# One hybrid decoder layer on one core: ScalarE and VectorE in program order through the mixer stage

## The chip, the core and the metric

The kernel runs on one core of a Trainium2 chip. Five engines of the core take part, each with its own row of instructions: TensorE (PE, matmuls; the profile shows its weight loads apart, as PEld), ScalarE (ACT), VectorE (DVE), GpSimd (POOL) and SyncE (SP, which issues nearly all transfers). An engine takes its row in the order in which it was built; an instruction that waits for a semaphore holds what stands behind it in that row. The metric is the time of one execution on the device in microseconds; lower is better. Two runs of the kernel before gave 2639.35 and 2638.07 us, median 2638.71.

## What is computed

One decoder layer (DEPTH is 1) over 2048 tokens of width 1024, all in float32. An input projection feeds two groups of four heads: gated DeltaNet (GDN) and HGRN2. Their outputs go through one output projection, then a squared-ReLU MLP, then a gated per-layer embedding. The gated delta rule solves a triangular system in each chunk of 64 tokens and carries a state of 128x128 from chunk to chunk; HGRN2 carries a state with a decay of its own for every row. The reference, cut to what matters:

```python
hn = rms_norm(h, pre_mix_norm[i])
proj = jnp.einsum('btd,dc->btc', hn, w_in[i]).astype(f32)
...
qkv = jax.nn.silu(causal_depthwise_conv(qkv, gdn_conv[i].astype(f32)))
q_a, k_a, v_a = jnp.split(qkv, 3, axis=-1)
...
o_a = gated_delta_rule_chunked(q_a, k_a, v_a, g_dec, beta)
o_a = gated_head_norm(o_a, gdn_norm[i], z_gdn)
...
log_f = jnp.logaddexp(jax.nn.log_sigmoid(f_pre), jnp.log(lb) + jax.nn.log_sigmoid(-f_pre))
k_b = (1.0 - lb) * jax.nn.sigmoid(-f_pre)
o_b = hgrn2_chunked(jax.nn.silu(q_hg), k_b, i_hg, log_f)
o_b = gated_head_norm(o_b, hgrn_norm[i], g_hg)
...
mix_out = jnp.einsum('btc,cd->btd', mix, w_out[i])
h = h + rms_norm(mix_out, post_mix_norm[i])

u = jnp.einsum('btd,df->btf', rms_norm(h, pre_mlp_norm[i]), w_mlp_up[i])
y = jnp.einsum('btf,fd->btd', jnp.square(jax.nn.relu(u)), w_mlp_down[i])
h = h + rms_norm(y, post_mlp_norm[i])

e = rms_norm(jnp.einsum('bte,ed->btd', p[i], w_ple_proj[i]), ple_norm[i])
gate = jax.nn.sigmoid(jnp.einsum('btd,de->bte', h, w_ple_gate[i]))
h = h + e * gate
```

## The kernel before

Every large float32 product is made of three matmuls on split operands: `split` (L174) writes a rounded copy of an array with ScalarE (L176, a copy) and the remainder with VectorE (L177, a subtraction that needs the copy), and TensorE multiplies high by high, high by low and low by high. `split_in_place` (L227) does the same where the array stands already (L229, L230).

The stages follow each other: a prologue (part of the embedding, the first input operands), the mixers, the output projection, the MLP, the gate. The change concerns the mixers. There the 2048 tokens are taken in four **quarters** of 512 tokens (index q, 0 to 3). In each quarter TensorE works through 33 **works**: a small one for the decay inputs, then for each of four heads h eight projections of 128 columns (`KINDS`: GDN's k, q, z and v, then HGRN2's f, i, q and g). A work is 24 matmuls of 128x512 on the input weights `w` and the input operands `xt` (L1176). In quarter 0 the weights of a work come raw from memory, are split and are kept in memory in split form (`stage_work`, `split_work`, `keep_work`, L1073 to L1086: transfers `raw`, then L176 and L177 on `w`, then `cache_in`); quarters 1 to 3 load the split form back (`reload`).

A clock of **ticks** ties the heads to the works. A work has three ticks of eight matmuls each (`SPT`), with a half-tick between. `tick` (L382) and `half` (L387) advance the generators that stand in `agenda` for that moment. `gdn_mixer` (L635) and `hgrn_mixer` (L857) are such generators: each `yield` ends a step, and the tables `A_STEPS` and `B_STEPS` (L56, L60) say at which tick, counted from the head's first work, a step is stated. So while TensorE projects one head, the scans of the head before are worked off in small pieces. In the GDN mixer the pieces that matter below are a triangular solve (`pr` and `xs`, L746 and L748, a chain of 30 VectorE instructions per head in which each needs the one before) and the recurrence over four chunks (`psa` on TensorE, `r` on VectorE L822, `psb` on TensorE, `w_g` on ScalarE L827, `psc` on TensorE, the new state `S_g` on VectorE L832). In the HGRN2 mixer there are seven levels; at each, VectorE scales the keys (L928), ScalarE copies them for TensorE (`keys`, L931), VectorE scales the queries (L932) and puts TensorE's product `at_all` into `att` (L933). Towards a quarter's end `load_x` (L1087) scales and splits the next quarter's operands `xt` (L1097, L176, L177), and `down_sums` forms sums of MLP weights. After the last quarter `early_outs` (L1047) begins the output projection (`mmo`) with its weights `w_out`.

Who sets the order in which an engine's instructions stand: inside `tc.manual_schedule(engines=...)` the named engines take them in the order in which the program states them; for every other engine the scheduler of the framework orders them by its own estimate of when their inputs are ready. TensorE is in program order in the whole kernel (L324). The prologue has SyncE, ScalarE and VectorE in program order too (L394). The mixer loop (L1156) has SyncE alone beside TensorE.

Of the kernel before, what the change touches and what calls it, by code (L numbers as in the profile page):

```python
# [96 lines left out]
def trunk(ctx, tc, x, xT, pT, vecs, w_in, w_ab, gdn_a_log, gdn_dt_bias, w_out, w_up, w_down,  # L97
# [13 lines left out]
    def bank(name, pool=None):  # L111
        return (pool or pm).tile([P, QT], F32, tag="ps", name=name)
# [269 lines left out]
    def tick():  # L382
        for gen in agenda.pop(clock[0], ()):
            next(gen, None)
        clock[0] += 1

    def half():  # L387

        for gen in agenda.pop(clock[0] - 0.5, ()):
            next(gen, None)  # L390
# [72 lines left out]
    with mixers as mctx:  # L463
# [60 lines left out]
        def decays(ps, q):  # L524

            sp = m2.tile([4, QT], F32, tag="tmp", name=f"sp_{q}")
            se = m2.tile([4, QT], F32, tag="th", name=f"se_{q}")
            S.activation(sp, ps[0:4, :], AF.Identity, bias=dec[:, 1:2])
            S.activation(gb[32:36, :], ps[32:36, :], AF.Tanh, scale=0.5)
            V.tensor_scalar(gb[32:36, :], gb[32:36, :], 0.5, 0.5, ALU.mult, ALU.add)  # L530
            V.scalar_tensor_tensor(se, sp, -1.0, sp, ALU.mult, ALU.max)
            S.activation(se, se, AF.Exp, scale=-1.0)
            S.activation(se, se, AF.Ln, bias=1.0)
            V.scalar_tensor_tensor(sp, sp, 0.0, se, ALU.max, ALU.add)
            V.tensor_scalar(sp, sp, nexpa, None, ALU.mult)
            for c in range(NC):
                V.tensor_tensor_scan(gb[0:4, blk(c)], one[0:4, :], sp[:, blk(c)], 0.0, ALU.mult, ALU.add)
            gd = dr.tile([4, QT], F32, name=f"gd{q}")
            decay[q] = [gd, None]
            yield  # L540
            nc.sync.dma_start(gd, gb[0:4, :])
            yield
            back = mt(f"gbb_{q}", "gbb", 1, (36, QT // 2))
            V.tensor_copy(back.rearrange("p (n b i) -> p n b i", b=NB, i=SB), odd_back(gb))
            yield
            ps = bank(f"ps_gb_{q}", ph)
            for c in range(NC):
                PE.transpose(ps[:, c * 36 : (c + 1) * 36], back[:, blk(c // 2)] if c % 2 else gb[:, blk(c)],
                             ident[:36, :36])
            gcol = sm.tile([P, NC, 36], F32, tag="gcol", name=f"gcol_{q}", bufs=2)  # L550
            V.tensor_copy(gcol.rearrange("p c n -> p (c n)"), ps[:, : NC * 36])
            V.tensor_scalar(gcol[:, :, 4:8], gcol[:, :, 0:4], -1.0, None, ALU.mult)
            decay[q][1] = gcol
# [459 lines left out]
        def at(t, gen, offsets):  # L1013
            for o in offsets:
                agenda.setdefault(t + o, []).append(gen)
# [31 lines left out]
        def early_outs():  # L1047

            for j, (q, d) in enumerate(order):
                for n in range(3, len(tile_of)):  # L1050
                    if ready_at(n) == j:
                        at(clock[0], ready_halves(n), (0, 1))
                for n in range(5, len(tile_of)):
                    if stage_at(n) == j:
                        stage_out(n)
                ps, w = bank(f"mmo_{q}_{d}"), ready[load_of[j]]
                for i in range(3 * KD):
                    k, term = i // 3, i % 3
                    PE.matmul(ps, w[:, term // 2, k, :], xin[q][k][:, term % 2, :], start=i == 0, stop=i == 3 * KD - 1)  # L1059
                    if i % 4 == 3 and i + 1 < 3 * KD:  # L1060
                        yield
                        while i > KD and held_y:
                            nc.sync.dma_start(*held_y.pop())
                y = m2.tile([P, QT], F32, tag="ld", name=f"yo{q}_{d}", bufs=2)
                S.activation(y, ps, AF.Copy)
                square_sums[q] = squares(square_sums[q], ps, d, f"o{q}")
                finished.append(j)
                held_y.append((yod[q][d], y))
                yield
# [3 lines left out]
        def stage_work(j):  # L1073

            if j < len(works) and works[j][3] == 0:
                staged[j] = stage(works[j][0], works[j][2])

        def split_work(j):

            if j < len(works):  # L1080
                split_w[j] = staged.pop(j)() if j in staged else reload(works[j][1], works[j][0])

        def keep_work(j):
            if works[j][3] == 0:
                keep(works[j][1], split_w[j])
# [67 lines left out]
        for q in range(2):  # L1153
            at(0, norm_steps(accs[q], 1.0 / D, EPS, f"e{q}", partial(ple_r.__setitem__, q)),
               [4 * q + i for i in (0, 2, 4, 5, 6)])
        with tc.manual_schedule(engines={mybir.EngineType.SP}):  # L1156
            stage_work(0)
            stage_work(1)
            split_work(0)
            stage_work(2)  # L1160
            split_work(1)
            for j, (name, key, src, q, h, then, g, b) in enumerate(works):
                split_work(j + 2)
                stage_work(j + 3)
                keep_work(j)
                ps = bank(f"mm_{name}")
                w, xt = split_w.pop(j), xts[q]
                terms = []
                for k, xk in enumerate(xt):
                    terms += [(w[:, 0, k, :], xk[:, 0, :]), (w[:, 0, k, :], xk[:, 1, :]), (w[:, 1, k, :], xk[:, 0, :])]  # L1170
                nt = len(terms)
                for s in range(SPT):
                    for i in range(s * nt // SPT, (s + 1) * nt // SPT):
                        if i == (2 * s + 1) * nt // (2 * SPT):
                            half()
                        PE.matmul(ps, *terms[i], start=i == 0, stop=i == nt - 1)  # L1176
                    if s == SPT - 1 and h is None:
                        at(clock[0], decays(ps, q), (0, 2, 3, 5) if q else (0, 2, 4, 7))
                    tick()
                    if s == SPT - 1 and h is not None:  # L1180
                        then(ps, q, h, g, b)

            outs = early_outs()
            while clock[0] <= last or len(finished) * SPT < clock[0] - end:
                next(outs)
                half()
                next(outs)
                tick()
            outs.close()
            nc.sync.dma_start(*held_y.pop())  # L1190
# [798 lines left out]
```

## Time and profile before

| | |
|---|---|
| median of two runs | 2638.71 us |
| span of the profiled execution | 2639.5 us |
| mixer loop, about | 46 us to 1030 us |
| VectorE busy over the span | 74% |
| ScalarE busy over the span | 55% |
| loads of ScalarE's function tables | 68 |

The profiled execution's own time is its span, 2639.5 us; it lies 0.15 us over the slower of the two runs, so nothing of weight lies around it. The page gives the busy time of each engine, the span in 40 slices of 66 us, the chain that ended last, and groups of instructions by line. Views of the trace used below are the busy time by stretch, the waits (which engine waited for what, in total, how often, longest), one line's instructions, and the timeline. In a row such as "128x512 f32 x3072 | 785.5, 401 | 1.6" stand the shape, the count, busy us in all and ns of one, and the engine's idle time before them. Matmuls overlap, so their mean is longer than the distance between them.

### The profile page before, as it was taken

The numbers are of one execution on the slowest core, as the hardware profiler recorded it, in microseconds if no ns is written. First come the engines' busy times: TensorE is split into PE (matmuls) and PEld (weight loads), VectorE is DVE, ScalarE is ACT, GpSimd is POOL, SyncE is SP. The second block draws the span as 40 slices with busy tenths as digits, with TensorE's granted clock in tenths as the row PEclk, the third lists the DMA queues.
The fourth block names the chain that finished last, engine by engine and source line by source line (L and its number), as shares of the span: only waits on it lengthen the run. The fifth ranks groups of instructions, "written<-read, shape, count | busy, mean of one in ns | idle before, by whom it ended". The sixth has DMA issues, their size and how long they took to land.

```text
span 2639.5 us, 43913 instructions
## 1 busy us (share of the span) xinstructions
PE 2602.8 (99%) x15593; PEld 2146.0 (81%) x15593; DVE 1965.0 (74%) x4032; ACT 1463.3 (55%) x2991; POOL 137.0 (5%) x147
## 2 busy tenths in 40 slices
PE   8999999999999999999999999999999999999999
PEld 6778788878878888787888888888888888888887
DVE  7778777776777777579988768767877765477775
ACT  7766655465555555566666465555454465565431
POOL 0000000000000000110000000001000001101000
PEclk9999999999999999999999999999999999999999
DMA  8877777767767675764675576665644375677663
GB/s 277 282 258 265 263 256 245 238 222 251 241 213 240 222 237 162 232 203 141 214 236 182 179 233 223 214 211 186 220 150 168 140 245 187 202 252 251 207 223 126
DMA packets 267788, 573.87 MB, mean 217 GB/s; under 512 B 55578, under 2 KB 60152, under 8 KB 250416
## 3 DMA queue, kind: packets, MB, share of 16 engines
q1 hardware_dynamic: 265264, 566.86, 64.5%
q0 software_dynamic: 2304, 4.20, 0.9%
q8 instruction: 123, 2.02, 0.3%
q14 instruction: 97, 0.79, 0.1%
HBM read 410.57 MB, written 160.37 MB: 216 GB/s over the span
## 4 chain that ended last, share of the span: by engine, by line
PE 61%; DMA 2%; issue 2%; DVE 2%; ACT 0%; POOL 0%; SPq 0%; DVEq 0%; POOLq 0%; ACTq 0%
PE d L1210 23%; PE u L1210 23%; PE mmg L1210 7%; PE mm L1176 4%; PE mmo L1059 1%; PE mme L203 1%; DMA yod<-yo 1%; DMA mixT<-mixd 0%; DMA rsb_g<-rd_g 0%; DMA yo<-in_xT_dram 0%; DVE t L177 0%; DMA rd_g<-m_g 0%; DVE acc_o L246 0%; POOL yo L1296 0%; DMA raw_out<-in_w_out_dram 0%
## 5 line engine op out<-in xcount | busy, mean ns | idle before, releaser
L1176 PE MATMUL mm<-xt,w 128*128 128x512 f32 x3072 | 785.5, 401 | 1.6 <-DVE acc_vg L571 0.7
L1176 PEld LDWEIGHTS mm<-xt,w 128*128 128x128 f32 x3072 | 552.8, 188 | 108.3 <-issue 2.1
L1210 PE MATMUL d<-db,da 128*128 128x512 f32 x2688 | 612.8, 389 | 0.0
L1210 PE MATMUL u<-t,wu 128*128 128x512 f32 x2604 | 591.2, 389 | 0.0
L1210 PEld LDWEIGHTS d<-db,da 128*128 128x128 f32 x2688 | 504.5, 188 | 104.8
L1210 PEld LDWEIGHTS u<-t,wu 128*128 128x128 f32 x2604 | 488.7, 188 | 101.5
L230 DVE TENSOR_TENSOR db<-db 128x512 fp32r<-128x512 f32 x224 | 159.5, 712 | 60.0 <-ACT db L229 59.0
L1612 DVE TENSOR_TENSOR u<-u,u 128x512 f32<-128x512 f32 x224 | 150.2, 681 | 52.0 <-PE u L1210 50.4
L229 ACT ACTIVATE db<-db 128x512 fp32r<-128x512 f32 x224 | 140.9, 629 | 67.4 <-DMA db<-hid 63.6
L1210 PE MATMUL mmg<-h2T,wg 128*128 128x512 f32 (+1 forms) x792 | 174.7, 383 | 0.0
L1210 PEld LDWEIGHTS mmg<-h2T,wg 128*128 128x128 f32 x792 | 145.5, 188 | 29.1
L1655 ACT ACTIVATE u<-u 128x512 f32<-128x512 f32 x128 | 80.7, 631 | 152.8 <-DVE u L1612 152.1
L177 DVE TENSOR_TENSOR da<-da 128x512 fp32r<-128x512 f32 x128 | 95.2, 743 | 91.3 <-ACT da L176 89.5
L176 ACT ACTIVATE da<-da 128x512 fp32r<-128x512 f32 x128 | 80.6, 630 | 127.8 <-DMA da<-sumd 100.9
L1210 PE MATMUL mmo<-mixT,w_out 128*128 128x512 f32 x600 | 140.0, 393 | 3.3 <-ACT w_out L176 2.0
L1210 PEld LDWEIGHTS mmo<-mixT,w_out 128*128 128x128 f32 x600 | 113.4, 190 | 28.8 <-DVE w_out L177 2.6
L176 ACT ACTIVATE wu<-a 128x512 fp32r<-128x512 f32 x124 | 75.0, 623 | 55.8 <-DMA a<-in_w_up_dram 52.9
L177 DVE TENSOR_TENSOR wu<-a,wu 128x512 fp32r<-128x512 f32 x124 | 85.9, 694 | 8.3 <-ACT wu L176 8.2
L177 DVE TENSOR_TENSOR da<-dr,da 128x512 fp32r<-128x512 f32 x96 | 68.2, 711 | 23.7 <-ACT da L176 22.2
L1656 ACT ACTIVATE u<-u 128x512 f32<-128x512 f32 x128 | 80.4, 628 | 3.0
L176 ACT ACTIVATE da<-dr 128x512 fp32r<-128x512 f32 x96 | 60.5, 630 | 31.9 <-DMA dr<-in_w_down_dram 21.7
L246 POOL TENSOR_TENSOR acc_y<-acc_y,sq_y 128x512 f32<-128x512 f32 x28 | 37.8, 1351 | 759.5 <-ACT sq_y L245 759.5
(401 smaller groups left out, 3675.4 us busy)
## 6 DMA issues: line engine op xcount, KB each, us to landing
w<-cache_in SPq DMA_DIRECT2D x96, 1024.0 KB
db<-hid SPq DMA_DIRECT2D x224, 256.0 KB
cache_in<-w SPq DMA_DIRECT2D x32, 1024.0 KB
hid<-u SPq DMA_DIRECT2D x128, 256.0 KB
da<-sumd SPq DMA_DIRECT2D x128, 256.0 KB
a<-in_w_up_dram SPq DMA_DIRECT2D x124, 256.0 KB
hid<-ht SPq DMA_DIRECT2D x96, 256.0 KB
dr<-in_w_down_dram SPq DMA_DIRECT2D x96, 256.0 KB
```

The lines of the kernel that those rows point to most:

```text
L176: S.activation(t[:, 0], raw, AF.Copy)
L177: eng.tensor_tensor(t[:, 1], raw, t[:, 0], ALU.subtract)
L203: PE.matmul(ps, a, b, start=i == 0, stop=i == n - 1)
L229: S.activation(t[:, 0], plain(t), AF.Copy)
L230: V.tensor_tensor(t[:, 1], plain(t), t[:, 0], ALU.subtract)
L246: eng.tensor_tensor(acc, acc, sq, ALU.add)
L1059: PE.matmul(ps, w[:, term // 2, k, :], xin[q][k][:, term % 2, :], start=i == 0, stop=i == 3 * KD - 1)
L1176: PE.matmul(ps, *terms[i], start=i == 0, stop=i == nt - 1)
L1210: PE.matmul(ps, a, b, start=start, stop=stop)
L1612: V.tensor_tensor(c[new], c[old], ps, ALU.add)
L1655: S.activation(c[k], c[k], AF.Relu)
L1656: S.activation(c[k], c[k], AF.Square)
```

## The change

One line: the mixer loop's scope names ScalarE and VectorE beside SyncE. Nothing is computed otherwise; no tile, buffer, transfer or step table is touched.

```diff
-        with tc.manual_schedule(engines={mybir.EngineType.SP}):
+        with tc.manual_schedule(engines={mybir.EngineType.SP, mybir.EngineType.Activation, mybir.EngineType.DVE}):
             stage_work(0)
             stage_work(1)
             split_work(0)
```

TensorE's row is the same instruction for instruction. ScalarE's and VectorE's rows hold the same instructions, among them 68 table loads as before, in another order through the mixer loop. GpSimd's and SyncE's rows change at a handful of places, for in the rest of the kernel the scheduler goes on from another state.

**ScalarE in quarter 0, second head's projections.** `w_16_0_1` is the split weight of the work that projects HGRN2's f for head 1; `keys_h0_0_2` and so on are the key copies of levels 2 and up of head 0. Before:

```order
L580 ACTIVATE y_qg0_1_1322<-acc_qg0_1_1315 128x512
L787 ACTIVATE part5_586<-psp5_g0_0_1395 32x2x32 x4
L931 ACTIVATE keys_h0_0_3_1417<-qk_h0_0_1011 128x2x8x16
L606 ACTIVATE zt_zg0_1_1426<-mm_12_0_1_1330 128x512
L685 ACTIVATE q2_g0_1_1494<-y_qg0_1_1322 128x512
L931 ACTIVATE keys_h0_0_4_1488<-qk_h0_0_1011 128x2x4x32
L176 ACTIVATE w_16_0_1_1323<-raw_16_0_1_1251 128x1024
```

and with the change:

```order
L567 ACTIVATE acc_qg0_1_1315<-mm_0_0_1_1255,cols_96 128x512
L568 ACTIVATE hist_581<-mm_0_0_1_1255 128x3
L176 ACTIVATE w_16_0_1_1323<-raw_16_0_1_1251 128x1024
L931 ACTIVATE keys_h0_0_2_1348<-qk_h0_0_1011 128x2x16x8
L500 ACTIVATE xs1_0_0_1265,ss2_x1_1264<-xs1_0_0_1265 128x512
L669 ACTIVATE jk_g0_1_0_1374,ssk_g0_1_1365<-t_kg0_1_1368 128x128
```

The weight's copy moved ahead, in front of three key copies behind which it stood.

**VectorE at the same place.** `att_h0_0` is the score array of head 0, `u_g0_1` and `qk_g0_1` belong to the GDN solve of head 1. Before:

```order
L932 TENSOR_TENSOR qk_h0_0_1011<-qk_h0_0_1011,gg_h0_0_2_1352 128x2x16x8
L933 COPY_PREDICATED att_h0_0_1207<-cst_93,at_all_81 128x2x16x8
L928 TENSOR_TENSOR qk_h0_0_1011<-qk_h0_0_1011,gg_h0_0_3_1421 128x2x8x16
L928 TENSOR_TENSOR qk_h0_0_1011<-qk_h0_0_1011,gg_h0_0_4_1492 128x2x4x32
L177 TENSOR_TENSOR w_16_0_1_1323<-raw_16_0_1_1251,w_16_0_1_1323 128x1024
L799 COPY xn_g0_0_1233<-psx5_g0_0_1459 32x2x32 x2
L932 TENSOR_TENSOR qk_h0_0_1011<-qk_h0_0_1011,gg_h0_0_3_1421 128x2x8x16
```

and with the change:

```order
L572 TENSOR_TENSOR acc_qg0_1_1315<-acc_qg0_1_1315,bound_582 128x3
L177 TENSOR_TENSOR w_16_0_1_1323<-raw_16_0_1_1251,w_16_0_1_1323 128x1024
L928 TENSOR_TENSOR qk_h0_0_1011<-qk_h0_0_1011,gg_h0_0_1_1302 128x2x32x4
L932 TENSOR_TENSOR qk_h0_0_1011<-qk_h0_0_1011,gg_h0_0_1_1302 128x2x32x4
L933 COPY_PREDICATED att_h0_0_1207<-cst_93,at_all_81 128x2x32x4
L939 TENSOR_TENSOR gg_h0_0_2_1352<-gg_h0_0_1_1302 128x64
L928 TENSOR_TENSOR qk_h0_0_1011<-qk_h0_0_1011,gg_h0_0_2_1352 128x2x16x8
L932 TENSOR_TENSOR qk_h0_0_1011<-qk_h0_0_1011,gg_h0_0_2_1352 128x2x16x8
```

Before, VectorE had two levels of key products done ahead of the weight's subtraction; now the subtraction stands ahead of level 1, and a level's instructions follow each other.

**VectorE at the turn to quarter 3.** `xt3_*` are quarter 3's input operands, `pr_g2_3` and `xs_g2_3` the solve of the last head of quarter 2, `r_g2_2_2` a step of a recurrence. Before:

```order
L748 TENSOR_REDUCE xs_g2_3_9417<-pr_g2_3_9416 128x4x2
L177 TENSOR_TENSOR xt3_2_9573<-raw_xt3_2_9439,xt3_2_9573 128x512
L746 TENSOR_TENSOR pr_g2_3_9416<-xs_g2_3_9417,sys_g2_3_9371 128x8x20
L177 TENSOR_TENSOR xt3_3_9576<-raw_xt3_2_9439,xt3_3_9576 128x512
L748 TENSOR_REDUCE xs_g2_3_9417<-pr_g2_3_9416 128x4x2
L614 TENSOR_TENSOR og_h2_2_9591<-of_h_86,zt_gh2_2_8876 128x512
L746 TENSOR_TENSOR pr_g2_3_9416<-xs_g2_3_9417,sys_g2_3_9371 128x8x22
L822 SCALAR_TENSOR_TENSOR r_g2_2_2_9589<-psa_g2_2_2_9587,tail_g2_2_8003,vt_g2_2_8695 128x128
```

and with the change:

```order
L746 TENSOR_TENSOR pr_g2_3_9416<-xs_g2_3_9417,sys_g2_3_9371 128x8x20
L748 TENSOR_REDUCE xs_g2_3_9417<-pr_g2_3_9416 128x4x2
L746 TENSOR_TENSOR pr_g2_3_9416<-xs_g2_3_9417,sys_g2_3_9371 128x8x22
L748 TENSOR_REDUCE xs_g2_3_9417<-pr_g2_3_9416 128x4x2
L177 TENSOR_TENSOR xt3_2_9573<-raw_xt3_2_9439,xt3_2_9573 128x512
L177 TENSOR_TENSOR xt3_3_9576<-raw_xt3_2_9439,xt3_3_9576 128x512
L822 SCALAR_TENSOR_TENSOR r_g2_2_2_9589<-psa_g2_2_2_9587,tail_g2_2_8003,vt_g2_2_8695 128x128
L614 TENSOR_TENSOR og_h2_2_9591<-of_h_86,zt_gh2_2_8876 128x512
```

Before, the steps of the solve alternated with independent work; now the solve's instructions, each of which needs the one before, stand back to back. Counted over both rows: VectorE instructions that wait for the VectorE instruction just ahead of them were 105 in quarter 0 and are 197 now, and in quarters 1 to 3 together 345 and 606.

## The prediction

> **What bounds the kernel now.** I read the page first: the span, the busy shares, the slices and the chain of work that ended last. The numbers in a slice row are tenths of the slice.
>
> ```profile
> span 2639.5 us, 43913 instructions
> PE 2602.8 (99%) x15593; PEld 2146.0 (81%) x15593; DVE 1965.0 (74%) x4032; ACT 1463.3 (55%) x2991; POOL 137.0 (5%) x147
> ...
> PE   8999999999999999999999999999999999999999
> ...
> DVE  7778777776777777579988768767877765477775
> ...
> PE 61%; DMA 2%; issue 2%; DVE 2%; ACT 0%; POOL 0%; SPq 0%; DVEq 0%; POOLq 0%; ACTq 0%
> ```
>
> TensorE is busy in 99% of the span, and of the chain it holds 61% against 2% for VectorE. So the span is TensorE's row of matmuls; the change leaves this row alone and can only take away or add waits in it. Next I took the busy time by stretch, one row for each quarter of the mixers (us, then PE, PEld, DVE, ACT, POOL busy, granted clock, DMA share, GB/s), and the waits of TensorE from 46 to 1070 us.
>
> ```profile
> 46.00:291.00 245.00, 239.47 (x1927) 196.38 (x1928) 192.32 (x512) 162.17 (x382) 13.94 (x24) 1.00 0.77 263
> 291.00:537.00 246.00, 242.78 (x2109) 200.44 (x2108) 185.78 (x544) 140.01 (x376) 15.93 (x18) 1.00 0.75 249
> 537.00:783.00 246.00, 242.83 (x2109) 200.71 (x2108) 182.97 (x539) 138.67 (x375) 14.62 (x17) 1.00 0.72 236
> 783.00:1030.00 247.00, 244.92 (x2199) 201.97 (x2198) 186.45 (x541) 138.36 (x377) 14.20 (x16) 1.00 0.70 224
> ```
>
> ```profile
> PE of_g L633 <- ACT y_qg L580: 2.5, 3, 1.0
> PE psa_g L820 <- DVE S_g L832: 1.9, 4, 0.6
> ...
> PE at_all L633 <- DVE att_h L933: 1.4, 4, 0.6
> ...
> PE nrm_g L284 <- DVE hl_g L177: 0.3, 1, 0.3
> ```
>
> TensorE stands idle 5.5 + 3.2 + 3.2 + 2.1 = 14.0 us in the four quarters, in many small waits. That is all that a better order could win here: 0.5% of the span. Nothing bounds the loss in the same way. VectorE is busy 192.3 of 245 us in quarter 0 (78%) and 183 to 186 of 246 after it (75%); ScalarE 66%, then 57%. The quarter where an order can go wrong is quarter 0, the only one that splits weights.
>
> **The change, part by part.** It removes nothing and adds no instruction. It moves instructions on ScalarE and VectorE, which now stand where the program states them. What is new is standing: an instruction whose input is not there holds the row behind it, where before the scheduler had put other work in front. Here are VectorE's waits in quarter 0, the two lines of the weight split, and two waits of ScalarE.
>
> ```profile
> DVE w L177 <- ACT w L176: 13.3, 11, 2.5
> DVE r_g L822 <- PE psa_g L820: 9.0, 5, 3.1
> ...
> DVE S_g L832 <- PE psc_g L830: 1.6, 3, 0.7
> ...
> DVE qk_h L932 <- PE at_all L915: 0.6, 1, 0.6
> ...
> DVE acc_kg L571 <- ACT hist L568: 0.2, 1, 0.2
> ```
>
> ```profile
> L176 ACT ACTIVATE w<-raw x31: 1042/1060/1066, 46.3 to 252.9; 128x1024 fp32r<-128x1024 f32 x31
> ...
> L177 DVE TENSOR_TENSOR w<-raw,w x31: 1185/1221/1227, 47.4 to 254.1; 128x1024 fp32r<-128x1024 f32 x31
> ```
>
> ```profile
> ACT w L176 <- DMA cache_in<-w: 14.7, 13, 2.8
> ...
> ACT keys_h L931 <- DVE qk_h L928: 1.2, 3, 0.8
> ```
>
> *Term 1, the weight splits of quarter 0.* The program states ScalarE's copy (1.06 us) and VectorE's subtraction (1.22 us) together, 31 times in this stretch. Before, 20 of the 31 subtractions did not wait at all, because other VectorE work stood between; all 31 together waited 13.3 us. Now both stand at the same place in their rows (the first two places shown with the change). When VectorE comes there no later than ScalarE, it stands for the copy, and behind it stand the key products that ScalarE's next key copy needs (wait of that kind before: 1.2 us in all); so the two engines hold each other in turn. The price of one is between 0 (VectorE is late, the copy is done) and the longest seen, 2.5 us. I take 13.3 / 11 = 1.2 us, the mean of those that did wait, as the nearest row: it is also about one copy. 31 x 1.2 = 37.2 us of standing.
>
> *Term 2, dependent neighbours on VectorE.* Two pieces of the timeline of VectorE (start, us, line) show what it costs that a step of the solve follows the step it needs.
>
> ```profile
> 102.68 0.41 DVE L746 TENSOR_TENSOR pr_g<-xs_g,sys_g 128x240 f32<-128x240 f32 x1
> 103.13 0.41 DVE L748 TENSOR_REDUCE xs_g<-pr_g 128x8 f32<-128x248 f32 x1
> ```
>
> ```profile
> 769.91 0.38 DVE L746 TENSOR_TENSOR pr_g<-xs_g,sys_g 128x208 f32<-128x208 f32 x1
> 770.20 0.69 DVE L177 TENSOR_TENSOR xt<-raw_xt,xt 128x512 fp32r<-128x512 f32 x1
> ```
>
> The dependent one starts 0.45 us after a start of 0.41 us length, 0.04 behind its end; the independent one starts 0.29 us after 0.38, 0.09 ahead of the end. The difference is 0.12 us. Such pairs grow by 92 in quarter 0 and by 261 in the three others: 92 x 0.12 = 11 us and 31 us, 10 a quarter. In quarters 1 to 3 VectorE has 60 us of idle time to put 10 us in, and I cost it at nothing; the cover goes where VectorE is full, which is term 3.
>
> *Quarter 0 as a sum.* VectorE's named waits in this stretch are 14 rows, from 13.3 down to 0.2, that add up to 47.7 us, so nearly all of its idle time (52.7 us) is standing for something: 13.3 for the splits, 11.2 for TensorE (9.0, 1.6 and 0.6), 23.2 for ScalarE, GpSimd and transfers. If VectorE runs late, TensorE's results are there when it comes and the 11.2 vanish; I let the 23.2 stay, since ScalarE is now in step with VectorE. Then 192.3 + 11 + 37.2 + 23.2 = 263.7 us against 245: **+18.7 us**. The ends: if the 23.2 vanish too, 240.5, which fits, +0; if everything stays, 274.9, +30. I take the middle one because ScalarE cannot run ahead any more. All of it comes out on TensorE, which waits for `att` (L933), `keys` and `w` within about one tick.
>
> *Term 3, the two later turns of a quarter and the start of the output projection.* Three stretches of 50 us, and the split of the operands.
>
> ```profile
> 500.00:550.00 50.00, 48.12 (x379) 38.83 (x378) 42.17 (x118) 27.67 (x59) 1.32 (x2) 1.00 0.70 239
> 750.00:800.00 50.00, 48.93 (x407) 39.39 (x407) 44.14 (x120) 29.81 (x72) 1.36 (x3) 1.00 0.69 231
> 1000.00:1050.00 50.00, 48.52 (x418) 39.79 (x417) 40.38 (x101) 28.66 (x65) 2.06 (x2) 1.00 0.49 146
> ```
>
> ```profile
> L176 ACT ACTIVATE xt<-raw_xt 128x512 fp32r<-128x512 f32 x24 | 14.7, 627 | 12.3 <-DVE raw_xt L1097 8.7 <-PE mm L1176 3.6
> ```
>
> At a turn VectorE is busy 42.2 and 44.1 of 50 us. Eight operand splits stand for a copy of 0.63 us each (5.0), dependent neighbours add 2.1 (10.1 x 50 / 246): 49.3 and 51.3 before any other standing. At 1000 to 1050 us there are some splits of `w_out` of the same kind and 40.4 us of work. The ends are 0 (the remaining idle vanishes) and 5 + 2.1 = 7.1 us each (all idle of before stays); I take 3 us each, under the middle since TensorE's waits leave about a tick: **+9 us**.
>
> *Parts that I cost at nothing.* The recurrence: VectorE stood 9.0 us for `psa` in quarter 0 already and `r` is stated right behind `psa`; the idle time between is its cover. Quarters 1 to 3 between the turns: no weight is split, and VectorE's 60 us of idle in each hide the 10 us of term 2; if the cover goes, the cost is at most those 10 us each. SyncE's row stays in program order; its transfers `raw` wait for VectorE's subtraction, two works ahead, and so are late only if VectorE is over a work (245 / 33 = 7.4 us) late, which is within rival one. GpSimd is busy 5%. After 1070 us the rows are scheduled as before.
>
> [...] After a wait of TensorE at 1113 us the granted clock fell (clock is the third column from the right):
>
> ```profile
> PE mmo L1210 <- ACT w_out L176: 2.0, 1, 2.0
> ```
>
> ```profile
> 1116.00:1118.00 2.00, 1.48 (x5) 0.90 (x4) 2.00 (x4) 0.64 (x2) 0.00 (x0) 0.72 1.11 262
> 1118.00:1120.00 2.00, 2.00 (x6) 1.58 (x5) 0.66 (x2) 0.63 (x1) 0.00 (x0) 0.50 1.10 287
> 1120.00:1122.00 2.00, 2.00 (x9) 1.61 (x8) 0.00 (x0) 1.42 (x3) 0.00 (x0) 0.93 1.04 379
> ```
>
> So 2.0 us of waiting were followed by (0.28 + 0.50 + 0.07) x 2 = 1.7 us of lost clock. [...]
>
> The sum: 18.7 + 9 = 27.7 us on the profiled execution's 2639.5 us, 2667 us. The span stands 0.8 us over the median of the runs (2638.71), which changes nothing.
>
> **The rivals.** *One: slower by over 2%.* Every split stands as long as the worst one did. ScalarE's copy itself waited for the store of the weight whose buffer it takes (14.7 us over 13, 2.8 at most); in the new row all that follows on ScalarE waits with it, and VectorE behind. Then term 1 is 31 x 2.5 = 77.5 us, quarter 0 takes 192.3 + 11 + 77.5 + 34.4 = 315 us instead of 245, +70, and with term 3 the time is 2718 us. It decides from a mean standing of 1.6 us a split: 192.3 + 11 + 34.4 + 31 x 1.6 = 287, +42, and with 9 the 2% are reached. For it speaks that ScalarE's own row waits for the same transfers; against it that a late VectorE finds its inputs ready.
>
> *Two: no slower.* The engines run late by less than a tick and TensorE never sees it: VectorE fits into quarter 0 with 240.5 of 245 us, and the waits that the estimated order caused go. Then the time is between 2639.5 - 14.0 = 2625.5 and about 2648, most likely that of before, 2640. For it speaks that key scores and states are now stated before unrelated work, so that TensorE's inputs move ahead in VectorE's row; against it the 78% of quarter 0.
>
> *Three: faster by over 2%.* The quarters hold 14.0 us of TensorE's idle time, the whole span 2639.5 - 2602.8 = 36.7; 2% are 52.8. It would need faster matmuls, which nothing in the rows offers.
>
> **How the numbers follow.** Forecast (2648 to 2691 us): 0.55, likeliest 2667. Rival one: 0.22. Rival two: 0.21. Rival three: 0.02. About 2% (2586 to 2691 us) is what a measurement of this kernel can tell from no change, so faster 0.02, same 0.55 + 0.21 = 0.76, slower 0.22. The range leaves out one in ten at each end: up to 2706, a little under half of rival one, and down to 2644, so that the upper part of rival two is in.
>
> **What would show it.** Right: VectorE's `w` (L177) waits for ScalarE's copy at nearly every split, some 30 to 40 us in all; the wait of `keys` for L928 grows from 1.2 us to tens; TensorE's idle time grows in quarter 0 by about 19 us, at `att` and `keys`, and hardly in quarters 1 to 3 away from the turns; VectorE's instructions L746 and L748 follow each other at their length plus 0.04 us. Wrong: quarter 0 takes 245 us as before (rival two), or quarters 1 to 3 each grow as much as quarter 0 (then it is not the weight split but the order of the heads' own steps), or the store of the weights is what ScalarE waits for (rival one).

## The result, and the profile after

| | before | after |
|---|---|---|
| median | 2638.71 us | 2725.94 us (2725.64 and 2726.24) |
| ratio, 95% interval | | 1.033 (1.030 to 1.036) |
| span of the profiled execution | 2639.5 us | 2723.9 us |

The change costs 87 us; +28 us was forecast, with 2706 as the upper end. The page of the profiled execution after:

```profile
span 2723.9 us, 43898 instructions
...
PE 2632.9 (97%) x15593; PEld 2161.6 (79%) x15593; DVE 1990.0 (73%) x4032; ACT 1459.9 (54%) x2991; POOL 137.0 (5%) x147
...
PE   7999899999999999899999999999999999999999
...
DVE  7677777786667766568989867767877775467775
...
PE 54%; DVE 2%; DMA 2%; issue 2%; ACT 1%; POOL 0%; SPq 0%; DVEq 0%; ACTq 0%; POOLq 0%
```

The two spans differ by 84.4 us. TensorE is idle 2723.9 - 2632.9 = 91.0 us instead of 36.7, which is 54.3; and its same 15593 matmuls are busy 30.1 us longer. The view of the granted clock tells where most of the 30 come from, first before, then after:

```profile
core 0: 2639.5 us, clock 0.999
```

```profile
core 0: 2723.9 us, clock 0.990
```

The clock lost is 0.001 x 2639.5 = 2.6 us before and 0.010 x 2723.9 = 27 us after, 24 to 25 us more. The share of VectorE hardly moved (74% to 73%), and its 40 slices look alike: from the busy shares nobody would guess that this engine is the cause.

Where the time goes is read by the works of the mixers. For each work the start of its first matmul (L1176) after is set against the same matmul before. These are differences of two rows of the trace, in us:

```
at the start of work         33     50     66     83     99    116    131    end
after                      25.0   33.2   39.5   48.1   58.1   64.5   76.2   84.4
```

Quarter 0 (works 0 to 32) loses 25 us, the first halves of the later quarters (works 33 to 50, 66 to 83, 99 to 116) 8.2 + 8.6 + 6.4 = 23 us, their second halves 6.3 + 10.0 + 11.7 = 28 us, and what follows work 131 loses 8 us. The busy time by stretch, with the bounds set at works 0, 33, 66 and 99, before:

```profile
40.00:275.50 235.50, 229.89 (x1838) 188.06 (x1839) 188.50 (x496) 158.13 (x377) 15.41 (x28) 1.00 0.78 266
275.50:520.90 245.40, 242.79 (x2109) 200.75 (x2108) 182.33 (x534) 139.44 (x375) 14.93 (x17) 1.00 0.76 253
```

and after:

```profile
40.00:300.50 260.50, 236.91 (x1839) 191.07 (x1840) 188.87 (x478) 155.27 (x375) 14.97 (x28) 0.98 0.73 241
300.50:560.40 259.90, 247.62 (x2109) 203.26 (x2108) 192.07 (x543) 138.26 (x376) 14.67 (x17) 0.99 0.71 239
```

In quarter 0 TensorE's idle time grows from 5.6 to 23.6 us, by 18.0; its busy time grows by 7.0. Quarter 1 has 12.3 us of idle time instead of 2.6. What TensorE waits for from 46 to 1070 us (us in all, times, longest):

```profile
PE psa_g L820 <- DVE S_g L832: 24.5, 13, 3.1
PE psa_g L820 <- DVE pr_g L746: 6.0, 3, 2.4
PE psc_g L830 <- ACT w_g L827: 4.2, 4, 1.7
PE psb_g L825 <- DVE r_g L822: 3.9, 1, 3.9
```

The wait for the state `S_g` of the recurrence stood for 1.9 us before. What VectorE waits for in the same stretch:

```profile
DVE r_g L822 <- PE psa_g L820: 55.9, 32, 2.6
DVE pr_g L730 <- DMA sys_g<-ud_g: 46.0, 11, 8.2
DVE w L177 <- ACT w L176: 39.7, 14, 5.6
```

The second of these is a wait that the prediction did not price. VectorE's timeline shows one of the eleven (start, us, line; the idle time before it in brackets):

```profile
734.36 0.18 DVE L729 COPY pr_g<-cst 128x64 f32<-128x64 f32 x1
742.76 0.28 DVE L730 TENSOR_TENSOR pr_g<-cst,sys_g 128x64 f32<-128x64 f32 x1 [8.22 <-DMA sys_g<-ud_g]
...
745.16 0.34 DVE L832 SCALAR_TENSOR_TENSOR S_g<-S_g,cd_g,psc_g 128x128 f32<-128x128 f32 x1
```

and TensorE's shows who waits:

```profile
738.94 0.39 PE L830 MATMUL psc_g<-w_g,kt_g 128*128 128x128 f32 x2
...
739.53 2.97 PE L1176 MATMUL mm<-xt,w 128*128 128x512 f32 x12
745.65 0.46 PE L820 MATMUL psa_g<-S_g,y_kg 128*128 128x128 f32 x2 [3.14 <-DVE S_g L832]
```

VectorE stands 8.2 us at the first step of the next head's solve (L730), whose system comes back from memory. That solve's result is needed some ticks later. Behind it in the row stand eight more instructions of the solve (2.4 us with the first) and only then the new state of the head before (L832), whose input `psc` TensorE had delivered at 739.3 and which TensorE would have used at 742.5 (745.65 - 3.14). It comes at 745.5.

### The profile page after: what moved, and what is told of

It is laid out like the page before. It is cut to its first block, busy times and chain, and to the rows that moved or that the text cites. A ratio compares the mean times of both kernels' runs of the same rounds, so it can differ in the third digit from the quotient of the medians.

```text
span 2723.9 us, 43898 instructions
## 1 busy us (share of the span) xinstructions
PE 2632.9 (97%) x15593; PEld 2161.6 (79%) x15593; DVE 1990.0 (73%) x4032; ACT 1459.9 (54%) x2991; POOL 137.0 (5%) x147
## 4 chain that ended last, share of the span: by engine, by line
PE 54%; DVE 2%; DMA 2%; issue 2%; ACT 1%; POOL 0%; SPq 0%; DVEq 0%; ACTq 0%; POOLq 0%
PE d L1210 22%; PE u L1210 22%; PE mmg L1210 6%; PE mmo L1059 1%; PE mme L203 1%; DMA mixT<-mixd 1%; DMA yod<-yo 1%; PE mm L1176 0%; DVE t L177 0%; DVE acc_o L246 0%; DVE mixT L230 0%; DMA yo<-in_xT_dram 0%; ACT mixT L229 0%; ACT sq_o L245 0%; DMA b<-h1d 0%
## 5 line engine op out<-in xcount | busy, mean ns | idle before, releaser
L1176 PE MATMUL mm<-xt,w 128*128 128x512 f32 x3072 | 801.4, 407 | 2.9 <-ACT qk_h L854 2.1
L1176 PEld LDWEIGHTS mm<-xt,w 128*128 128x128 f32 x3072 | 564.2, 192 | 112.1 <-ACT qk_h L854 2.6
L931 ACT ACTIVATE keys_h<-qk_h 128x256 f32<-128x256 f32 x80 | 33.4, 418 | 111.3 <-DVE qk_h L928 110.8
```

The lines of the kernel that those rows point to most:

```text
L931: S.activation(keys.rearrange("p (n a s) -> p a n s", a=2, s=2 * s), side(k, QT, 2 * s, False), AF.Copy)
```

## The experiments

A theory was formed from these rows. **A**: instructions that are stated before their input is there (the solve before its transfer, the weight's subtraction before its copy) hold urgent ones behind them. Its rivals have letters in the expectations. All times are medians, and ratios are to the kernel before on the same chip. Lateness is given at works 33, 50, 66, 83, 99, 116 and 131, as above.

### Which engine carries it

```diff
-engines={mybir.EngineType.SP, mybir.EngineType.Activation, mybir.EngineType.DVE}
+engines={mybir.EngineType.SP, mybir.EngineType.Activation}    # act_alone
+engines={mybir.EngineType.SP, mybir.EngineType.DVE}           # dve_alone
```

> Only ScalarE (beside SyncE) is taken in program order through the mixer loop; VectorE is ordered by the scheduler as before. Theory A (what costs is VectorE's row, where the new state S_g stands behind a solve that waits for its transfer): ScalarE's order alone costs part of quarter 0 at most, 2640 to 2655 us, TensorE's wait psa <- S_g stays near 2 us. Rival B (the two engines hold each other, so either one in program order is enough): 2680 us or more.

> Only VectorE (beside SyncE) is taken in program order; ScalarE is ordered by the scheduler. Theory A: the waits psa <- S_g of quarters 1 to 3 are all there (some 25 us, with the slower clock behind them), quarter 0 loses less than with both, 2695 to 2720 us. Rival B (it takes both engines in step): below 2670 us.

ScalarE alone: 2657.0 us, 1.0062 (1.0046 to 1.0079). VectorE alone: 2728.6 us, 1.0334 (1.0317 to 1.0351), which is the whole change and above the 2720 us expected. TensorE's largest wait with VectorE alone is the same one, from 46 to 1070 us:

```profile
PE psa_g L820 <- DVE S_g L832: 28.8, 16, 3.5
```

So it is VectorE's row, and the two engines in step are not needed for it. ScalarE alone cost a little more than the 2655 us expected.

### Steps stated before their transfer

`solve_half_later` states the solve's first step behind the state that stood behind it. `steps_spaced` does the like for the solve, the next quarter's operands and the first operands of the output projection; `steps_spaced_scheduled` is the same tables with the scheduler's order. Two shorter waits for transfers are still there (from 40 to 1125 us `m_g` L293 has 9.7 us and `raw_xt` L1097 7.5 us, after 7.5 and 3.4 in the changed kernel), and no run states them later. (The four transposes of `v` move with the solve's first step.)

```diff
-A_STEPS = ((3, 6, 7, 8, 9, 10, 12, 14) + tuple(range(16, 24)) + ...
+A_STEPS = ((3, 6, 7, 8, 9, 10, 12, 14, 16.5) + tuple(range(17, 24)) + ...             # solve_half_later
+A_STEPS = ((3, 6, 7, 8, 9, 10, 12, 14) + (19, 19.5, 20, 20.5, 21, 21.5, 22, 23) + ... # steps_spaced
-at(end, mix_operands(0), (-14, -11, -3, -3, -2, -2, -1, -1))
+at(end, mix_operands(0, 2), (-14, -11, -3, -3, -2, -2, -1, -1, -1, -1))
-at(per_q * q, load_x(q), range(-9, 0))
+at(per_q * q, load_x(q), (-14, -11, -10, -8, -6, -4, -3, -2, -1))
```

> Both engines in program order; the solve's first step (L730, which waits for the transfer sys) is stated half a tick later, behind the state S_g of the head before, at tick 16.5 instead of 16. Theory A: the six lone waits psa <- S_g that follow a wait for sys go, with the clock lost behind four of them (1.6 + 1.5 + 4.2 + 5.0 + 2.2 + 4.0 = 18.5 us of lateness), 2700 to 2708 us, and psa <- S_g falls from 27.2 us to 12 or less. Rival C (VectorE is simply too full with dependent neighbours, and something else holds S_g next): 2718 to 2730 us.

> Both engines in program order, and the steps that were seen standing for a transfer are stated later than its issue: the solve from tick 19 on instead of 16, the next quarter's operands loaded at tick -14 and scaled from -11 on instead of -9 and -8, the first operands of the output projection split two steps behind their load. Quarter 0's weight splits stay as they are. Theory A (instructions stated before their transfer is there hold the states S_g): quarters 1 to 3 lose less than half of the 51 us that they lose now, psa <- S_g falls from 27 us under 12 us, 2685 to 2702 us. Rival C (VectorE is too full for program order at all): the waits move again and the time stays at 2715 us or more.

> The kernel before, ScalarE and VectorE ordered by the scheduler, with the same step tables as steps_spaced: what the tables do by themselves. All theories: the scheduler had already put the work behind its transfers, so 2635 to 2650 us.

`solve_half_later`: 2726.7 us, no change. Its lone waits for `S_g` went, as theory A had it, but not the time. VectorE now came early to the operands of the next quarter and stood there instead, and ScalarE's `w_g` (behind another such step) was late next. VectorE, then TensorE, from 40 to 1125 and from 46 to 1070 us:

```profile
DVE raw_xt L1097 <- DMA raw_xt<-in_xT_dram: 22.6, 3, 9.6
DVE pr_g L730 <- DMA sys_g<-ud_g: 12.0, 8, 2.8
```

```profile
PE psa_g L820 <- DVE S_g L832: 11.2, 8, 2.2
PE psc_g L830 <- ACT w_g L827: 11.2, 7, 2.1
PE psa_g L820 <- DVE pr_g L729: 10.5, 3, 4.0
```

`steps_spaced`: 2719.3 us, 1.0296 (1.0280 to 1.0313). The tables by themselves do nothing: 2643.4 us, 1.000 (0.9991 to 1.0010). In program order they move the loss:

```
at the start of work         33     50     66     83     99    116    131
after                      25.0   33.2   39.5   48.1   58.1   64.5   76.2
solve_half_later           29.5   36.7   44.3   50.5   61.7   65.9   76.2
steps_spaced               33.9   45.6   46.3   55.9   56.5   65.0   66.0
```

The second halves of quarters 1 to 3 lose 0.7 + 0.6 + 1.0 = 2.3 us instead of 28. The waits for `sys` are down from 46.0 us to 0.4. This part is settled; the solve's first step alone (`solve_half_later`) did not do it. But the first halves lose 30 us instead of 23, and quarter 0 loses 34 instead of 25. Behind work 131 `steps_spaced` loses another 13 us where the changed kernel loses 8, so that of its lead of 10 us there 5 are left at the end. The time hardly moves: theory A's 2702 was missed, and 2719 is in the range that rival C named.

### Quarter 0

`split_later` states the weight's subtraction two tick ends behind its copy; `split_mid_work` states the pair one tick into the work; `steps_spaced_split_later` is `split_later` on top of `steps_spaced`; `q0_scheduled` opens the changed scope at work 33 only. `split_unlinked` takes the dependence away and with it leaves out the low part of quarter 0's weights.

```diff
                 S.activation(w[:, 0], raw, AF.Copy)
-                V.tensor_tensor(w[:, 1], raw, w[:, 0], ALU.subtract)
+                at(clock[0], rest(w), (1,)) if clock[0] else next(rest(w))   # split_later; rest(w) is the subtraction
+                V.tensor_scalar(w[:, 1], raw, 0.0, None, ALU.mult)           # split_unlinked
```

```diff
-                split_work(j + 2)
+                if j + 2 >= len(works) or works[j + 2][3]: split_work(j + 2)
...
-                    tick()
+                    tick(); s == 0 and j + 2 in staged and split_work(j + 2)   # split_mid_work
```

> Both engines in program order; in quarter 0 the subtraction of a weight split is stated two tick ends behind its copy instead of right behind it. Theory A (term 1 of the prediction): VectorE's 40.6 us of waiting for the copies of w fall under 10 us, and 10 to 18 us come back in quarter 0: 2708 to 2716 us. Rival D (the copies and the key steps hold each other in any case): the waiting moves to the key copies, 2721 to 2728 us.

> As steps_spaced, and in quarter 0 the subtraction of a weight split two tick ends behind its copy. Theory A: alone this edit was slower because VectorE then came earlier to the transfer of the solve; with the solve stated later it gives back 8 to 15 us of quarter 0, 2672 to 2692 us. Rival D (copies and key steps hold each other in any case): within 4 us of steps_spaced, or slower.

> Both engines in program order; in quarter 0 a work's weight is split one tick into the work two ahead of it, not at its start, so that the store that frees its buffer and its load have 2.5 us more. Theory A (ScalarE's copy stands 12.6 us for transfers, VectorE 40.6 us for the copies): VectorE's waits for w fall under 25 us, works 0 to 33 are late by 15 us or less instead of 25, 2708 to 2717 us. Rival D (both engines meet at a pair that is stated together in any case): 2721 us or more.

> Quarter 0 (works 0 to 32) with ScalarE and VectorE in the scheduler's order as before, quarters 1 to 3 in program order as in the changed kernel. If the quarters' losses are independent: the 25 us of quarter 0 come back, 2697 to 2706 us. If the later quarters' loss comes from VectorE being late at the end of quarter 0: 2690 us or less. If the scheduler's order gives trouble where the two meet: 2710 us or more.

> The changed kernel, but VectorE writes zeros (raw times 0) where the remainder of a weight of quarter 0 stood, in the same place of its row: it does not need ScalarE's copy, so VectorE cannot stand for it. The low part of quarter 0's weights, and what the later quarters load back of it, is left out of the computation. Theory A (term 1): works 0 to 33 are late by 12 us or less instead of 25, 2705 to 2716 us. Rival D (whatever VectorE does not stand for there, it stands for at the next step of its row): 2720 us or more, with VectorE waiting for the solve's transfer instead.

| | time, us | ratio, interval | late at work 33, us |
|---|---|---|---|
| split_later | 2737.0 | 1.0359 (1.0338 to 1.0379) | 35.2 |
| steps_spaced_split_later | 2720.9 | 1.0308 (1.0290 to 1.0326) | 33.5 |
| split_mid_work | 2725.4 | 1.0318 (1.0303 to 1.0334) | 23.0 |
| q0_scheduled | 2702.5 | 1.0237 (1.0222 to 1.0253) | -1.6 |
| split_unlinked | 2713.7 | 1.0272 (1.0248 to 1.0296) | 14.0 |

Quarter 0's share is its own: without it the later quarters lose as much as before (56.0 us from work 33 to 131, after 51.2). In `split_later` VectorE was freed from the copies and stood for the solve's transfer instead, 81.0 us over the mixers, and got slower. `steps_spaced_split_later` changed nothing against `steps_spaced` (2720.9 and 2719.3). `split_mid_work` gave VectorE 35.9 us of waiting for copies instead of 40.6, and nothing in the time. Only without the dependence does quarter 0 gain, 11 us; not all of it need be the standing, for the instruction that takes the subtraction's place is also shorter (0.69 us against 1.22, 32 times). Theory A's "12 us or less" at work 33 was just missed, its time was met.

### The turn of a quarter

`urgent_first` states the first HGRN2 step and the boundary terms behind the state at the turn. `spaced_urgent_mid` is `steps_spaced`, `urgent_first` and `split_mid_work` together. `decays_spread` adds to it the decay chain in three steps.

```diff
-            call(per_q * q, boundary)
+            call(per_q * q + 1, boundary)
-B_STEPS = (24, 26, ...
+B_STEPS = (24.5, 26, ...
-at(clock[0], decays(ps, q), (0, 2, 3, 5) if q else (0, 2, 4, 7))                        # decays_spread
+at(clock[0], decays(ps, q), (0, 1.5, 2.5, 3, 4, 5) if q else (0, 0.5, 1, 2, 4, 7))      # with a yield around Exp and Ln
```

> Both engines in program order; at the turn of a quarter the first HGRN2 step (L875 to L880, 2.1 us of VectorE) is stated half a tick later and the convolution's boundary terms (L558 to L562) one tick later, both behind the state S_g that stood behind them. The load stays the same. Theory H (urgent steps stand behind work that is not needed yet): the waits psa <- S_g of 2.2 us behind the three turns go, with the clock lost behind them (3.4, 5.0 and 3.8 us), 2710 to 2716 us. Rival I (VectorE is late there anyway): 2721 us or more.

> steps_spaced with urgent_first and split_mid_work. If the three places are what program order costs here: 2680 to 2700 us (steps_spaced was 2719). If what is taken away at one place only shows the next: 2708 us or more.

> spaced_urgent_mid, and at the turn the chain of the decay inputs (L528 to L537: ScalarE, VectorE, two table loads, ScalarE, VectorE) is stated in three steps over 2.5 ticks instead of at once, with the recurrence's copy w_g (L827) ahead of its middle part. If what is left at the turns are such steps: the waits psc <- w_g and at_all behind it (some 2.4 us a turn) go, 2704 to 2710 us. If the next step takes their place: 2713 us or more.

`urgent_first`: 2725.8 us, no change; `spaced_urgent_mid`: 2714.7, 1.0281 (1.0264 to 1.0298); `decays_spread`: 2719.9, 1.0306 (1.0289 to 1.0323). The wait that `urgent_first` aimed at went, at each turn. TensorE's waits at the first turn in the changed kernel (297 to 328 us; the 2.2 us end at 310.3):

```profile
PE psa_g L820 <- DVE S_g L832: 2.2, 1, 2.2
PE psx_g L633 <- ACT osq_g L286: 0.7, 1, 0.7
PE mm_ab L1176 <- DVE xt L177: 0.3, 1, 0.3
```

and in `urgent_first` (300 to 330 us):

```profile
PE psc_g L830 <- ACT w_g L827: 1.4, 1, 1.4
PE psa_g L820 <- DVE S_g L832: 1.2, 1, 1.2
PE at_all L633 <- DVE att_h L933: 0.9, 1, 0.9
```

Of these, the 1.2 us of `psa` stand at 301.1, ahead of the turn; at the turn itself `psa` no longer waits. In place of the 2.2 us, two smaller waits came behind it, 1.4 and 0.9 us, 2.3 together. In `decays_spread` these two were gone in their turn, and a wait of 3.0 to 3.1 us for the decay chain itself (`ps_gb` for `gbb`) came at each turn. That VectorE's row as a whole is late at the turns, and not one step of it, fits this; it is argued and not shown.

### Work taken from VectorE

The weights' subtractions (`split_on_gpsimd`), the operands' row factor at the turns (`spaced_scale_gpsimd`, on `steps_spaced`) and both (`spaced_both_gpsimd`; `scheduled_both_gpsimd` with the scheduler's order) go to GpSimd.

```diff
-                split(w, V, raw)
+                split(w, G if clock[0] else V, raw)
-                V.scalar_tensor_tensor(raws[k], raws[k], col(R_PREMIX + k), rsb, ALU.mult, ALU.mult)
+                G.tensor_tensor(raws[k], raws[k], rsb, ALU.mult)    # the column factor in the copy and the subtraction
```

> Both engines in program order; in quarter 0 GpSimd, not VectorE, does the subtraction of a weight split. VectorE neither stands for the copies nor spends 1.22 us on each. Theory A (term 1): works 0 to 33 are late by 12 us or less instead of 25, 2708 to 2716 us. Rival H (a queue in program order has no priority: what is freed is spent on standing for the next transfer, as in split_later): 2722 us or more, with more waiting at pr <- sys.

> As steps_spaced, and at the turns GpSimd multiplies the operands by the row factor (a column factor goes into ScalarE's copy and VectorE's subtraction), so that VectorE has eight instructions of 0.74 us less at each turn. Theory H (at the turns the states S_g queue behind a full VectorE; no transfer is left there): the three waits psa <- S_g of 2.2 us behind the turns go with the clock that they cost, 2700 to 2710 us. Rival I (dependent neighbours by themselves): 2714 us or more.

> As spaced_scale_gpsimd, and the weight subtractions of quarter 0 on GpSimd too. Theories A and H together (standing for inputs, and urgent steps behind a full queue): works 0 to 33 late by 15 us or less (34 in steps_spaced), the later quarters by 20 in all, 2675 to 2695 us. If program order costs by itself, whatever the load: 2706 us or more.

> The kernel before (scheduler's order) with the same work moved to GpSimd: what the move does by itself. TensorE bounds it, so 2630 to 2645 us.

2722.9, 2716.5 and 2713.0 us, and 2671.0 with the scheduler's order, where 2645 at most was expected: 1.0124 (1.0101 to 1.0146), so the move itself costs 1.2%. A likely reason is seen on VectorE in `scheduled_both_gpsimd`, and at the same time on GpSimd, whose subtraction also takes 2.39 us against VectorE's 1.22:

```profile
116.40 1.99 DVE L932 TENSOR_TENSOR qk_h<-qk_h,gg_h 128x256 f32<-128x256 f32 x1
```

```profile
115.71 2.39 POOL L177 TENSOR_TENSOR w<-raw,w 128x1024 fp32r<-128x1024 f32 x1 [4.18 <-ACT hist L568]
```

An instruction of 0.42 us took 1.99 us and ended 0.3 us behind GpSimd's. From 40 to 310 us 31 of VectorE's instructions are longer by over 0.3 us than the median of their kind in the kernel before, by 44 us together; before it is one, by 1.4 us. Why VectorE's instructions take longer there is not shown. So quarter 0 was not relieved by these runs, and they do not tell whether VectorE's load is the cause there. At the turns `spaced_scale_gpsimd` lost as much as `steps_spaced` (32 us in the first halves, against 30). It relieved VectorE little there: 24 instructions of 0.74 us, 17.8 us, went away, and those that ran beside GpSimd's multiplications were 12.6 us longer than the median of their kind before.

### The clock

`clock_probe` is the kernel before with 36 waits of TensorE made on purpose, each of 1 to 12 GpSimd copies.

```diff
                         PE.matmul(ps, *terms[i], start=i == 0, stop=i == nt - 1)
+                        if i == 12 and j in PROBES:
+                            for _ in range(PROBES[j]):
+                                G.tensor_copy(terms[i][1][:, :PW], terms[i][1][:, :PW])
```

> The kernel before with 36 waits of TensorE made on purpose, two works apart from work 36 on: GpSimd copies 128 columns of the operand in use onto itself 1 to 12 times, and the next matmul on it waits. Theory F (the traces: every wait up to 1.96 us left the clock alone, 13 of 14 waits of 2.14 us and more were followed by 3.4 us at half clock): the clock falls behind the waits of over 2.1 us and behind none under 1.9 us, and each fall costs 1.7 us. [...]

Its span is 2776.7 us, at a mean clock of 0.982. All 18 probes of 2.78 us and more were followed by half clock, of five from 2.05 to 2.55 us two were, and one of the shorter ones (1.69 us). Theory F's bound of about 2 us holds for the long waits, but three of five just above it left the clock alone. What decides there is the last section's subject.

## Why the prediction was wrong, by its own steps

The direction was right and the size was not. By the prediction's terms, with the lateness of the works that they speak of:

| term | forecast, us | measured, us |
|---|---|---|
| quarter 0 (works 0 to 32) | 18.7 | 24.9 |
| turn to quarter 2 (works 62 to 68) | 3 | 7.7 |
| turn to quarter 3 (works 95 to 101) | 3 | 7.8 |
| output projection (work 128 to the end) | 3 | 15.1 |
| quarters 1 to 3 elsewhere | 0 | 28.8 |
| sum | 27.7 | 84.3 |

**What bounds it**, and that a faster result is not to be had: right as far as the runs go: none of the versions that were run beat the kernel before. That the change "can only take away or add waits" in TensorE's row was not all of it: 24 of the 84 us are clock (below).

**Term 1** was right in its mechanism, and its size came out by luck: 37.2 us of standing for the copies forecast, 40.6 measured (40 to 300 us). The forecast had 31 waits of 1.2 us, "at nearly every split"; there were 15, of 2.7 us in the mean and 5.6 at most, and the other splits did not wait. The two engines hold each other as foretold, as ScalarE's wait for `keys` shows, which was 1.2 us before:

```profile
ACT keys_h L931 <- DVE qk_h L928: 32.3, 12, 4.1
```

That this standing costs the quarter's time is shown only in part: `split_unlinked`, without it and with 17 us less work, brings 11 of the 25 us back.

**Quarter 0's sum** forecast 18.7 us of waiting; TensorE's idle time grew by 18.0. The 7 us on top lie in its busy time, 5.1 of them in three windows at half clock. That the 18 were met is again partly luck, for the forecast path, TensorE waiting for `att`, `keys` and `w`, does not occur: from 40 to 300.5 us none of these three is in the list of its waits. It begins:

```profile
PE psc_g L830 <- ACT w_g L827: 4.0, 3, 1.7
PE at_all L915 <- ACT y_vg L577: 3.2, 2, 1.6
PE nrm_e L284 <- DVE hl_e L177: 3.2, 2, 2.4
PE psa_g L820 <- DVE S_g L832: 3.0, 2, 2.7
```

The third of these, with another 2.0 us of `nrm_e` for ScalarE's `hl_e`, stands in the first works: the operands `hl_e` of the embedding's norm stand behind weight splits there, and on VectorE the second ones also behind the decay inputs. By the start of work 3 the kernel is 6.8 us late. No experiment moves this step by itself.

**Term 2** was too large: VectorE's busy time grew by 9.7 us in quarter 1 (182.3 to 192.1), where 10 was forecast, but by 0.4 in quarter 0 (188.5 to 188.9), where 11 was, and by 25.0 over the whole span (1965.0 to 1990.0), where 42 was. What it costs in time is not decided by a run.

**The parts costed at nothing** are the step that failed: "VectorE stood 9.0 us for `psa` in quarter 0 already and `r` is stated right behind `psa`; the idle time between is its cover". The cover was counted over a whole quarter (60 us of idle time), but in program order that idle time stands ahead of urgent work and cannot be used by it. A row of the kernel before showed the danger: `pr_g L730 <- DMA sys_g<-ud_g` had 5.0 us in quarter 0. The prediction kept it among the waits that stay and did not ask what would stand behind it. From 46 to 1070 us TensorE then waited 24.5 us for `S_g`, and `steps_spaced` shows that steps stated before their transfer were nearly the whole loss of the second halves (28 us, and 2.3 without them). The prediction had named the sign: quarters 1 to 3 growing as much as quarter 0 would speak for the order of the heads' own steps. To the start of work 131 they grew by 14.5, 18.6 and 18.1 us, quarter 0 by 25.0.

**Term 3** had the right place and was mis-sized: 3 us each against 7.7, 7.8 and 15.1. Its mechanism was the smaller part: from 530 to 580 us VectorE stands 1.4 us for the copies of `xt`, where 5.0 were priced, while TensorE waits 3.1 and 2.2 us for `S_g` and runs 10.2 us at half clock. In the third place, 6.9 us (by the start of work 130) are the first operands `mixT`, which were split in the step of their load, with VectorE standing 7.9 us; `steps_spaced` lost 1.0 us from work 116 to 131 where the changed kernel lost 11.7, but from work 128 to the end it still lost 13.1 where the changed kernel lost 15.1.

**The clock** has no term in the sum, and 24 of the 84 us are clock. By the row that the prediction itself quoted, a wait of 2.0 us cost 1.7 us of clock; half clock stood in 15 windows of 3.41 us behind 13 waits of 2.1 to 3.9 us in the mixers and the output projection, 15 x 3.41 / 2 = 25.6 us; the kernel before had one such window, 1.7 us. The sum holds only if the added waits leave the clock alone, and these 13 did not.

**Rival one** named 2718 us, the nearest of all, but by luck. It asked for a mean standing of 2.5 us a split, behind ScalarE's waits for the store `cache_in`; the standing was 40.6 / 31 = 1.3 us, and the waits for that store fell from 14.7 to 10.1 us.

**What stays open**: 25 us of quarter 0 (11 of them tied to the splits), 23 us in the first halves, and the 8 us behind work 131. In the first two every step that was restated brought the next to light, and no version with VectorE in program order and with all its work came below 2713 us but the one that left quarter 0 out. That VectorE has no spare time there in program order, so that what one step gains the next one waits, fits these runs but is not shown: no run had much less work for VectorE at the turns, and a rule for which order would do was not found.

## What to carry to other kernels

An engine that is busy three quarters of the time (here VectorE, 73% of the span) can still set the end when it takes its work in the order of the text: its idle time then lies in front of instructions that wait (8.2 us at one step of the solve), and urgent ones stand behind them. Before pinning an engine's order, go through its row and ask at each wait for a transfer or for another engine what stands behind it and who needs that; and price a wait of TensorE of well over 2 us at its length plus at least 1.7 us (here all 18 added waits of 2.78 us and more were followed by half clock, and two of the five from 2.05 to 2.55 us). When a wait is taken away and the time stays, look for the next wait in the same row before trusting or dropping the theory.

## What the runs showed of the hardware

The clock falls by windows. In five traces (the changed kernel, `dve_alone`, `split_later`, `steps_spaced`, `clock_probe`) the half clock that follows a wait always lasts 3.41 us or twice that, and in each its starts lie on one grid of 3.413 us. With the windows of the changed kernel set on that grid (bounds, length, PE busy; the granted clock is third from the right):

```profile
678.62:682.03 3.41, 1.02 (x5) 0.58 (x4) 3.24 (x10) 1.25 (x2) 0.00 (x0) 1.00 0.99 392
682.03:685.44 3.41, 3.41 (x14) 3.12 (x14) 1.88 (x8) 0.00 (x0) 0.00 (x0) 0.50 1.00 401
...
```

```profile
804.90:808.31 3.41, 2.13 (x10) 1.44 (x8) 1.99 (x6) 0.09 (x1) 0.00 (x0) 1.00 1.02 378
808.31:811.72 3.41, 1.74 (x13) 1.69 (x14) 2.73 (x8) 0.54 (x1) 0.00 (x0) 1.00 0.59 209
811.72:815.13 3.41, 3.41 (x18) 2.84 (x17) 2.60 (x8) 1.54 (x4) 0.00 (x0) 1.00 0.19 59
```

A wait of 2.4 us inside one window (idle 2.39 us) halves the next one; a longer wait of 2.9 us that falls on two windows (1.28 and 1.67 us) costs nothing more. Over the five traces, from 40 to 1125 us, all 64 windows at full clock with 1.95 us of idle time or more, 57% of a window, were followed by half clock, and 2 of the 56 with 1.2 to 1.9 us. The lost clock is lost time: in `clock_probe` TensorE's idle time grew by 91.6 us and the busy time of its same matmuls by 45.6, and the lost clock, taken from the granted clock of the two traces, is 0.018 x 2776.7 - 0.001 x 2639.5 = 47 us.
